# Plain weight pieces dealt in another order among the seven-product pairs of a one-core decoder block

## The chip, the core and the metric

The kernel runs on one core of a Trainium2 chip. The time is the device time of one execution in microseconds (us). Before the change it was 1505.64 us, the median of three runs (1503.54 to 1506.01).

The engines are named as in the profile: PE is TensorE (matmuls), DVE is VectorE, ACT is ScalarE, POOL is GpSimd, and SP is the engine whose queue issues the weight loads. Each engine works through its instructions in the order in which they were queued.

## The reference

A decoder block on 256 tokens of width 2048, in float32: one projection `w_in`, gated linear attention beside a short gated convolution, a merge by gates, an output projection, and a SwiGLU feed-forward part with 5632 hidden columns. What the change touches are the order of the gate projections and of the SwiGLU part.

```python
def hybrid_mixer(h, w_in, ...):
    proj = jnp.einsum('bsd,de->bse', h, w_in)
    (q, k, v, g_out, gk_low, gate_b, gate_c, xc, merge_a, merge_b) = jnp.split(proj, ...)
    ...
    y_a = o * jax.nn.silu(g_out)
    y_b = gate_b * causal_depthwise_conv(gate_c * xc, conv_w)
    merged = jax.nn.sigmoid(merge_a) * y_a + jax.nn.sigmoid(merge_b) * y_b
    return jnp.einsum('bse,ed->bsd', merged, w_out)

def swiglu(h, w_gate_up, w_down):
    gate, up = jnp.split(jnp.einsum('bsd,df->bsf', h, w_gate_up), [FFN_HIDDEN], axis=-1)
    return jnp.einsum('bsf,fd->bsd', jax.nn.silu(gate) * up, w_down)
```

## The kernel before

**Pieces.** All weights come as pieces of 128 x 1024 float32 (512 KB): two blocks of 128 rows by 512 columns. Each piece is split in two parts that TensorE takes at full speed: ScalarE rounds it (`hi`, line 238) and VectorE forms the remainder (`lo` = piece - `hi`, line 243). A product is then three matmuls (`mm3`, lines 347 to 349), with `lo` in the first. A *plain* piece is used for both halves of the 256 tokens: 2 blocks x 2 halves x 3 = 12 matmuls of 512 columns.

**Pairs.** Where two weight matrices meet the same input (`gc` and `xc` of the gates, `fg` and `fu` of SwiGLU), a pair of 512-column blocks is computed with seven products instead of eight. It has 28 pieces of 6 matmuls. `seven_list` gives their order: four quarters (q = 0 to 3) of five pieces `11`, `t1`, `t3`, `t2`, `t4`, and then eight last pieces `21` and `22`. The `t` pieces are sums of weight blocks: VectorE adds them (`sum_of`, lines 259 and 265), `t3`, `t2` and `t4` in place in the tile `x`; then the sum is rounded by ScalarE, and its `lo` formed by VectorE. The next sum in `x` needs the `lo` of the one before. `t2` is formed of what is there and needs no load. When a pair's products are complete, VectorE combines them with `v2`, `v3` and `u` (lines 424 to 437).

**Order.** `gates_list` and `hidden_list` write down the order of all pieces by hand. Among the 28 pieces of a pair stand plain pieces of other products. The gate pairs `gc0`, `gc1` and `gc2` have 24 plain pieces each (three products of eight), `gc3` has 32; the SwiGLU pairs of blocks 3, 5 and 7 have 16, those of blocks 4, 6, 9 and 10 have 15 (table `SEVENS`). The plain pieces there are, in order, those of `fg1`, `fu1`, `fg2`, `fu2`, of the down projection `dn0_0` to `dn1_3`, of `fg8`, `fu8`, and of `dn2_0` to `dn2_3`. The SwiGLU pair of block 0 has a table of its own.

`mixed` deals the plain pieces: one behind each `t` piece, then one behind each of the last eight, and round again while there are any. With 24 each quarter has four and each of the last eight one; with 16 or 15 the quarters take all, and the last eight stand in a row.

**Running ahead.** `take` emits the loading of five pieces ahead of their use (`LOOK`); there are five buffers for raw pieces, six for `hi`, five for `lo`. So VectorE can be some pieces ahead of TensorE. Steps that follow a product (evictions, transposes, the gates' elementwise work) are queued a given number of pieces later (`later`, `one_at_a_time`). Three PSUM banks serve the plain products (`lent`), two for one product, one for each half of the tokens; so a product that follows another takes over, for its second half, the bank of the other's first half, and it must have been drained by then: the gates `g` and `gb` by ScalarE (lines 929 and 935), `ma` and `mb` by ScalarE and VectorE (lines 919 and 920), the down projection by VectorE (`h`, line 1103). A scheduler may still move single instructions on their engines.

Of the kernel before, what the change touches and what calls it, by code (L numbers as in the profile page):

```python
# [19 lines left out]
KC = D // P  # L20
# [23 lines left out]
def plan():  # L44
# [28 lines left out]
GATES = (  # L73
    (None, ("g0",)),
    (("gc0", "xc0"), ("ma0", "gb0", "mb0")),
    (("gc1", "xc1"), ("g1", "ma1", "gb1")),
    (("gc2", "xc2"), ("mb1", "g2", "ma2")),
    (("gc3", "xc3"), ("gb2", "mb2", "g3", "ma3")),
    (None, ("gb3", "mb3")),
)  # L80
# [3 lines left out]
FIRST = {0: (6, 6, 8, 10, 12), 1: (14, 14, 16, 18, 20), 2: (22, 22, 23, 24, 26), 3: (28, 28, 29, 30, 31)}  # L84
FIRST_END = (31, 32)
SEVENS = ((3, 16), (4, 15), (5, 16), (6, 15), (7, 16), (9, 15), (10, 15))
PLAIN = (1, 2, (0, (0, 1, 2)), (1, (3, 4, 5)), 8, (2, (6, 7, 8)))


# [10 lines left out]
def seven_list(pair):  # L100

    out = [(what, q) for q in range(4) for what in ("11", "t1", "t3", "t2", "t4")]
    twos = (("21", 0), ("21", 1), ("22", 0), ("21", 2), ("22", 1), ("21", 3), ("22", 2), ("22", 3))
    return [(pair, e) for e in out + list(twos)]


def mixed(pair, eights, early=False):

    if pair is None:
        return eights  # L110
    sevens = seven_list(pair)
    sums = ("t1", "t3", "t2", "t4")
    gaps = [0] * len(sevens)
    rest = len(eights)
    while rest > 0:
        for some in (sums + ("11",) if early else sums, ("21", "22")):
            for n, (_, e) in enumerate(sevens):
                if e[0] in some and rest > 0:
                    gaps[n] += 1
                    rest -= 1  # L120
    out, put = [], 0
    for e, n in zip(sevens, gaps):
        out += [e] + eights[put:put + n]
        put += n
    return out


def gates_list():
    return [e for pair, keys in GATES
            for e in mixed(pair, [(key, k) for key in keys for k in range(0, KC, 2)], keys[0] == "gb2")]  # L130


def block_of(key):
# [3 lines left out]
def down_of(part, n, f):  # L137

    first = 4 * (f - PARTS[part][0])
    return [(f"dn{part}_{n}", k) for k in range(first, first + 4, PIECE // DOWN[part][n][1])]  # L140


def hidden_list():

    plain = []
    for what in PLAIN:
        if isinstance(what, tuple):
            part, fs = what
            plain += [e for n in range(len(DOWN[part])) for f in fs for e in down_of(part, n, f)]
        else:  # L150
            plain += [(f"{name}{what}", k) for name in ("fg", "fu") for k in range(0, KC, 2)]
    plain = [(f"wo{n}", k) for n in range(1, 4) for k in range(0, KC, 2)] + plain

    before = {(what, q): FIRST[q][n] for q in range(4) for n, what in enumerate(("11", "t1", "t3", "t2", "t4"))}
    pair = seven_list(("fg0", "fu0"))
    for n, (_, e) in enumerate(pair[20:]):
        before[e] = FIRST_END[0] + n * (FIRST_END[1] - FIRST_END[0]) // 7
    out, put = [], 0
    for key, e in pair:
        out += plain[put:before[e]] + [(key, e)]  # L160
        put = before[e]
    plain = plain[put:]
    for f, n in SEVENS:
        out += mixed((f"fg{f}", f"fu{f}"), plain[:n])
        plain = plain[n:]
    return out + plain

# [9 lines left out]
def stream_list():  # L177

    pieces = [(p[0], p[3]) for p in piece_list()]
    out = [e for e in pieces if e[0][0] in "kqv"] + gates_list() + [e for e in pieces if e[0] == "wo0"]  # L180
    return out + hidden_list() + down_list()
# [3 lines left out]
def block_kernel(ctx, tc, x, xt, cols_in, gkw_in, gku_in, gnw, conv_w, finw, w_in, w_out, w_gu, w_dn, out):  # L185
# [790 lines left out]

    xy = None
    steps = run(gates_list(), begin_gate)
    for n in steps:
        if n == 2:  # L980
# [82 lines left out]

    act = {}
    order = hidden_list()

    base = count["tick"]
# [178 lines left out]
```

## Time and profile before

| | |
|---|---|
| median of three runs | 1505.64 us |
| the profiled execution | 1504.77 us |
| its span, first to last instruction | 1503.1 us |
| granted TensorE clock, mean | 0.999 |
| ScalarE busy | 862.9 us (57%) |
| GpSimd busy | 37.9 us (3%) |
| HBM read | 351.03 MB |

A row of the profile names the line of the kernel, the engine, the operation, the tile that is written and those that are read, and where rows are grouped their count. In rows in order of time the first column is the start in us from the span's start and the second the duration in us. A matmul's row lasts longer than its share of the pace, since matmuls overlap: what counts is the distance from start to start. Behind an idle time stands, in square brackets, what ended it.

### The profile page before, as it was taken

How to read it: one execution, taken by the hardware profiler on the slowest of the kernel's cores; microseconds unless marked ns; L12 is line 12 of the kernel's file. 1: busy time of each engine (PE TensorE's matmuls, PEld its weight loads, DVE VectorE, ACT ScalarE, POOL GpSimd, SP SyncE). 2: the span in 40 equal slices, each digit the busy share in tenths (PEclk: the TensorE clock that was granted, in tenths of full speed). 3: DMA queues.
4: the chain of work that ended last, by engine and by line, in shares of the span. 5: the costliest groups of instructions: out<-in, count | busy, mean ns of one | idle time of the engine just before them, and what ended most of it. 6: DMA issues, size and time to landing. Idle time of an engine off the chain costs nothing.

```text
span 1503.1 us, 19369 instructions
## 1 busy us (share of the span) xinstructions
PE 1489.3 (99%) x7064; PEld 1243.9 (83%) x7064; DVE 1277.8 (85%) x1283; ACT 862.9 (57%) x977; POOL 37.9 (3%) x60
## 2 busy tenths in 40 slices
PE   9999999999999999999999999999999999999998
PEld 8989988888888888888888888888888788888887
DVE  6775869979979878966689999999999999999975
ACT  7773546655654654654556756655565556565553
POOL 0030000000000000000000000000000000000000
PEclk9999999999999999999999999999999999999999
DMA  9655557876886977786666777777877778777782
GB/s 354 200 170 179 171 170 265 273 230 232 281 259 235 304 227 252 258 264 209 217 220 214 238 246 251 255 261 220 272 238 239 253 263 269 246 263 231 235 287 94
DMA packets 100127, 358.57 MB, mean 239 GB/s; under 512 B 11492, under 2 KB 11620, under 8 KB 99904
## 3 DMA queue, kind: packets, MB, share of 16 engines
q1 hardware_dynamic: 96656, 346.73, 70.8%
q0 software_dynamic: 2800, 8.89, 2.2%
q10 hardware_dynamic: 576, 1.72, 0.3%
q8 instruction: 55, 0.90, 0.2%
q14 instruction: 40, 0.33, 0.1%
HBM read 351.03 MB, written 2.10 MB: 235 GB/s over the span
## 4 chain that ended last, share of the span: by engine, by line
PE 89%; DVE 5%; issue 3%; ACT 2%; DMA 1%; SPq 0%; DVEq 0%; ACTq 0%
PE fg L347 7%; PE fg L349 7%; PE fg L348 7%; PE dn L347 5%; PE dn L349 5%; PE dn L348 5%; PE gc L347 3%; PE gc L348 3%; PE gc L349 3%; DVE lo L243 3%; PE wo L347 2%; PE v L347 2%; PE v L348 2%; PE gb L347 2%; PE gb L349 2%
## 5 line engine op out<-in xcount | busy, mean ns | idle before, releaser
L243 DVE TENSOR_TENSOR lo<-raw,hi 128x1024 fp32r<-128x1024 f32 (+1 forms) x506 | 612.5, 1218 | 109.1 <-ACT hi L238 28.0
L238 ACT CAST hi<-raw 128x1024 fp32r<-128x1024 f32 (+1 forms) x506 | 523.8, 1047 | 270.8 <-PE gb L349 26.4
L238 ACT CAST hi<-x 128x1024 fp32r<-128x1024 f32 x144 | 151.6, 1053 | 276.2 <-DVE x L265 211.0
L243 DVE TENSOR_TENSOR lo<-x,hi 128x1024 fp32r<-128x1024 f32 x144 | 176.2, 1223 | 36.1 <-ACT hi L238 26.1
L347 PE MATMUL dn<-lo,acth 128*128 128x512 f32 (+1 forms) x368 | 140.8, 383 | 1.8 <-DVE h L1103 1.0
L349 PE MATMUL dn<-hi,acth 128*128 128x512 f32 (+1 forms) x368 | 139.9, 380 | 0.0
L348 PE MATMUL dn<-hi,actl 128*128 128x512 f32 (+1 forms) x368 | 139.8, 380 | 0.0
L265 DVE TENSOR_TENSOR x<-x,raw 128x1024 f32<-128x1024 f32 x96 | 117.1, 1220 | 14.7 <-DMA raw<-in_w_in_dram 9.3
L347 PE MATMUL fg<-lo,hh 128*128 128x512 f32 x288 | 112.4, 390 | 0.0
L348 PE MATMUL fg<-hi,hl 128*128 128x512 f32 x288 | 112.2, 389 | 0.0
L349 PE MATMUL fg<-hi,hh 128*128 128x512 f32 x288 | 112.2, 389 | 0.0
L347 PE MATMUL fg<-lo,sh 128*128 128x512 f32 x256 | 101.0, 395 | 0.0
L348 PE MATMUL fg<-hi,sl 128*128 128x512 f32 x256 | 99.9, 390 | 0.0
L349 PE MATMUL fg<-hi,sh 128*128 128x512 f32 x256 | 99.8, 390 | 0.0
L347 PEld LDWEIGHTS dn<-lo,acth 128*128 128x128 f32 x368 | 69.2, 188 | 16.2 <-DVE h L1103 2.3
L349 PEld LDWEIGHTS dn<-hi,acth 128*128 128x128 f32 x368 | 69.2, 188 | 13.3
L348 PEld LDWEIGHTS dn<-hi,actl 128*128 128x128 f32 x368 | 69.3, 188 | 12.9
L347 PEld LDWEIGHTS fg<-lo,hh 128*128 128x128 f32 x288 | 54.1, 188 | 11.8 <-DVE lo L243 0.5
L349 PEld LDWEIGHTS fg<-hi,hh 128*128 128x128 f32 x288 | 54.1, 188 | 11.2
L348 PEld LDWEIGHTS fg<-hi,hl 128*128 128x128 f32 x288 | 54.1, 188 | 11.1
L243 DVE TENSOR_TENSOR lo<-y,hi 128x1024 fp32r<-128x1024 f32 x48 | 58.5, 1219 | 5.4 <-ACT hi L238 2.4
L259 DVE TENSOR_TENSOR raw<-y,x 128x1024 f32<-128x1024 f32 x48 | 58.6, 1220 | 3.0 <-DMA y<-in_w_in_dram 1.5
(247 smaller groups left out, 3068.1 us busy)
## 6 DMA issues: line engine op xcount, KB each, us to landing
raw<-in_w_in_dram SPq DMA_DIRECT2D x254, 512.0 KB, 4.6
raw<-in_w_gu_dram SPq DMA_DIRECT2D x176, 512.0 KB, 4.4
raw<-in_w_dn_dram SPq DMA_DIRECT2D x88, 512.0 KB, 4.5
x<-in_w_gu_dram SPq DMA_DIRECT2D x32, 512.0 KB, 4.9
y<-in_w_gu_dram SPq DMA_DIRECT2D x32, 512.0 KB, 3.8
raw<-in_w_out_dram SPq DMA_DIRECT2D x32, 512.0 KB, 3.7
y<-in_w_in_dram SPq DMA_DIRECT2D x16, 512.0 KB, 4.2
x<-in_w_in_dram SPq DMA_DIRECT2D x16, 512.0 KB, 4.9
```

The costliest lines, as they stand in the source:

```text
L238: nc.scalar.copy(hi[:, ks, :], raw[:, ks, :])
L243: nc.vector.tensor_tensor(out=lo[:, ks, :], in0=raw[:, ks, :], in1=hi[:, ks, :].bitcast(F32), op=ALU.subtract)
L259: nc.vector.tensor_tensor(out=raw, in0=y, in1=held["x"], op=ALU.add)
L265: nc.vector.tensor_tensor(out=x, in0=x, in1=other, op=ALU.add)
L347: nc.tensor.matmul(ps, lhsT=sh, rhs=ml, start=first, stop=False, skip_group_check=onto)
L348: nc.tensor.matmul(ps, lhsT=sl, rhs=mh, start=False, stop=False, skip_group_check=onto)
L349: nc.tensor.matmul(ps, lhsT=sh, rhs=mh, start=False, stop=last, skip_group_check=onto)
```

## The change

The dealing is no longer done by one rule but by two tables of numbers, which say how many plain pieces each quarter gets; a quarter gives them out behind its pieces in the order `t1`, `t3`, `t2`, `t4`, `11`, `t3`, `t2`, and what is left is spread evenly over the last eight. In a gate pair with 24 the quarters get 5, 6, 6 and 5 instead of four each, and the last eight 2 instead of 8; with 32 the quarters get 7, 7, 7 and 6 and the last eight 5, where the quarters had 9, 5, 5 and 5 and the last eight 8. In a SwiGLU pair the quarters get 4, 4, 3 and 3 (16 plain pieces) or 4, 4, 3 and 2 (15), and the last eight 2, where they had none. The two stand in the middle of the last eight and at the end. The pair of block 0 and all that is outside the pairs stay.

```diff
+GATES_QUADS = {24: (5, 6, 6, 5), 32: (7, 7, 7, 6)}
+SEVENS_QUADS = {15: (4, 4, 3, 2), 16: (4, 4, 3, 3)}
...
+def dealt(pieces, quads):
+
+    out = []
+    for n in quads:
+        places = [0] * 5
+        for i in (1, 2, 3, 4, 0, 2, 3)[:n]:
+            places[i] += 1
+        out += places
+    rest = pieces - sum(quads)
+    return out + [(i + 1) * rest // 8 - i * rest // 8 for i in range(8)]
+
+
-def mixed(pair, eights, early=False):
+def mixed(pair, eights, gaps):
 
     if pair is None:
         return eights
-    sevens = seven_list(pair)
-    sums = ("t1", "t3", "t2", "t4")
-    gaps = [0] * len(sevens)
-    rest = len(eights)
-    while rest > 0:
-        for some in (sums + ("11",) if early else sums, ("21", "22")):
-            for n, (_, e) in enumerate(sevens):
-                if e[0] in some and rest > 0:
-                    gaps[n] += 1
-                    rest -= 1
+    assert sum(gaps) == len(eights)
     out, put = [], 0
-    for e, n in zip(sevens, gaps):
+    for e, n in zip(seven_list(pair), gaps):
         out += [e] + eights[put:put + n]
         put += n
     return out
...
-        out += mixed((f"fg{f}", f"fu{f}"), plain[:n])
+        out += mixed((f"fg{f}", f"fu{f}"), plain[:n], dealt(n, SEVENS_QUADS[n]))
```

Two places show what becomes of this on the engines. The first is VectorE's queue in the fourth quarter of the SwiGLU pair of block 6, from the addition of `t3` on: the tile `x` holds the sums `t3`, `t2` and `t4` one after the other, `lo` from `raw` is that of a plain piece, and `h` is the draining of `dn1_1`. Before:

```order
L265 TENSOR_TENSOR x_9835<-x_9835,raw_9867 128x1024
L243 TENSOR_TENSOR lo_9872<-raw_9849,hi_9850 128x1024
L243 TENSOR_TENSOR lo_9884<-x_9835,hi_9870 128x1024
L243 TENSOR_TENSOR lo_9901<-raw_9880,hi_9881 128x1024
L265 TENSOR_TENSOR x_9835<-x_9835,y_9817 128x1024
L243 TENSOR_TENSOR lo_9914<-x_9835,hi_9899 128x1024
L243 TENSOR_TENSOR lo_9927<-raw_9910,hi_9911 128x1024
L265 TENSOR_TENSOR x_9835<-x_9835,raw_9922 128x1024
L1103 TENSOR_TENSOR h_6297<-dn1_1_0_9743,h_6297 128x512
L1103 TENSOR_TENSOR h_6297<-dn1_1_1_9744,h_6297 128x512
L243 TENSOR_TENSOR lo_9947<-x_9835,hi_9925 128x1024
```

With the change (the lines of the file are nine higher):

```order
L274 TENSOR_TENSOR x_9817<-x_9817,raw_9849 128x1024
L252 TENSOR_TENSOR lo_9872<-x_9817,hi_9852 128x1024
L252 TENSOR_TENSOR lo_9883<-raw_9868,hi_9869 128x1024
L274 TENSOR_TENSOR x_9817<-x_9817,y_9805 128x1024
L252 TENSOR_TENSOR lo_9892<-x_9817,hi_9881 128x1024
L274 TENSOR_TENSOR x_9817<-x_9817,raw_9894 128x1024
L1112 TENSOR_TENSOR h_6297<-dn1_1_0_9743,h_6297 128x512
L1112 TENSOR_TENSOR h_6297<-dn1_1_1_9744,h_6297 128x512
L252 TENSOR_TENSOR lo_9909<-x_9817,hi_9897 128x1024
```

The `lo` of `t3` now stands directly behind the addition that makes `t3`, where a plain piece's `lo` stood between them; the plain piece between `t2` and `t4` is gone, so that the addition of `t4` follows the `lo` of `t2` at once.

The second place is TensorE's queue in the gate pair `gc0`, where the plain product `ma0` ends (`ma0_1` is its second half of the tokens). Before:

```order
L347 MATMUL ma0_1_2352<-lo_2523,xh_108 128x512
L348 MATMUL ma0_1_2352<-hi_2508,xl_109 128x512
L349 MATMUL ma0_1_2352<-hi_2508,xh_108 128x512
L347 MATMUL gc0_0_2321<-lo_2543,xh_108 128x512
L348 MATMUL gc0_0_2321<-hi_2521,xl_109 128x512
L349 MATMUL gc0_0_2321<-hi_2521,xh_108 128x512
```

With the change:

```order
L356 MATMUL ma0_1_2341<-lo_2499,xh_108 128x512
L357 MATMUL ma0_1_2341<-hi_2484,xl_109 128x512
L358 MATMUL ma0_1_2341<-hi_2484,xh_108 128x512
L356 MATMUL gb0_0_2577<-lo_2516,xh_108 128x512
L357 MATMUL gb0_0_2577<-hi_2496,xl_109 128x512
L358 MATMUL gb0_0_2577<-hi_2496,xh_108 128x512
```

Before, two pieces of the pair (`11` and `t1` of its third quarter) stood between `ma0` and the next plain product `gb0`; now `gb0` begins directly behind it. The same holds for `g1` and `ma1` in `gc1`, `mb1` and `g2` in `gc2`, and `g3` and `ma3` in `gc3`.

More of the change, by code (lines that the diff above doesn't have):

```diff
@@ L128, in gates_list @@
 def gates_list():
-    return [e for pair, keys in GATES
-            for e in mixed(pair, [(key, k) for key in keys for k in range(0, KC, 2)], keys[0] == "gb2")]
+    out = []
+    for pair, keys in GATES:
+        eights = [(key, k) for key in keys for k in range(0, KC, 2)]
+        out += mixed(pair, eights, dealt(len(eights), GATES_QUADS[len(eights)] if pair else ()))
+    return out
 def block_of(key):
```

## The prediction

> **What bounds the kernel now.** I read the busy times first, then the chain that ended last, then one row per pair, and then single instructions.
>
> ```profile
> span 1503.1 us, 19369 instructions
> ...
> PE 1489.3 (99%) x7064; PEld 1243.9 (83%) x7064; DVE 1277.8 (85%) x1283; ACT 862.9 (57%) x977; POOL 37.9 (3%) x60
> ...
> PE 89%; DVE 5%; issue 3%; ACT 2%; DMA 1%; SPq 0%; DVEq 0%; ACTq 0%
> ```
>
> TensorE (PE) holds 89% of the chain, and VectorE (DVE) 5%: there are places where PE waits for it. The change leaves every matmul as it is, so only PE's stalls can move. To size them I take the pace from PE's rows in order of time: the starts of two pieces of the pair `gc1` with a plain piece of `g1` behind the first.
>
> ```profile
> 349.38 0.39 PE L347 MATMUL gc<-lo,sh 128*128 128x512 f32 x1
> ...
> 353.46 0.39 PE L347 MATMUL gc<-lo,sh 128*128 128x512 f32 x1
> ```
>
> These 18 matmuls take 4.08 us: 2.72 for the 12 of a plain piece, 1.36 for the 6 of a pair piece. Below is the table of stretches, each from the start of one pair to that of the next: four gate pairs, then the SwiGLU pairs of blocks 3, 4, 5, 6, 7, 9 and 10.
>
> ```profile
> core 0: us, PE busy (x) PEld busy (x) DVE busy (x) ACT busy (x) POOL busy (x), PEclk, DMA share, GB/s
> 227.01:330.57 103.56, 103.56 (x457) 85.51 (x456) 89.90 (x81) 62.54 (x65) 0.00 (x0) 1.00 0.78 255
> 330.57:435.81 105.24, 104.89 (x465) 86.35 (x464) 95.91 (x90) 60.81 (x64) 5.01 (x9) 1.00 0.78 257
> 435.81:542.03 106.22, 105.15 (x465) 86.07 (x464) 93.92 (x87) 60.02 (x63) 4.95 (x9) 1.00 0.78 255
> 542.03:668.20 126.17, 126.17 (x561) 104.25 (x560) 105.47 (x97) 70.58 (x74) 5.07 (x10) 1.00 0.81 256
> 865.02:948.55 83.53, 83.53 (x377) 69.14 (x376) 77.98 (x74) 50.73 (x54) 0.00 (x0) 1.00 0.77 250
> 948.55:1028.89 80.34, 80.34 (x361) 66.50 (x360) 75.80 (x72) 45.53 (x48) 0.00 (x0) 1.00 0.76 251
> 1028.89:1112.03 83.14, 83.14 (x373) 68.68 (x372) 77.56 (x75) 46.84 (x50) 0.00 (x0) 1.00 0.76 252
> 1112.03:1193.34 81.31, 80.74 (x357) 65.80 (x356) 76.65 (x74) 45.34 (x48) 0.00 (x0) 1.00 0.77 252
> 1193.34:1277.32 83.98, 83.10 (x370) 68.29 (x368) 78.89 (x76) 46.72 (x50) 0.00 (x0) 1.00 0.77 251
> 1277.32:1358.53 81.21, 81.21 (x365) 66.73 (x364) 76.28 (x72) 48.39 (x52) 0.00 (x0) 1.00 0.79 254
> 1358.53:1440.32 81.79, 80.42 (x358) 65.92 (x356) 76.69 (x75) 46.29 (x49) 0.00 (x0) 1.00 0.74 241
> ```
>
> The pieces alone need 28 x 1.36 plus 2.72 for each plain piece: 103.36 us with 24, 125.12 with 32, 81.60 with 16, 78.88 with 15. Records beyond the pieces' own matmuls are transposes; block 4's row (361 - 348 = 13 of them, 80.34 - 78.88 = 1.46 us) prices them at 0.11 us, if it has no stall. The rest of each stretch is stall: 0.1, 0.9, 1.9 and 0.1 in the gates (2.9 together), and 0.1, 0, 0.1, 1.4, 1.3, 0.5 and 1.8 in SwiGLU (5.2, of which 5.1 from block 5 on). So **8 us is all that a better order could win here**. The clock is 1.00 in all rows. PE's waits name the releasers:
>
> ```profile
> PE dn L347 <- DVE h L1103: 1.0, 2, 0.5
> PE trb L597 <- DVE sg L1062: 0.9, 1, 0.9
> PE dn L347 <- DVE lo L243: 0.8, 1, 0.8
> PE ma L347 <- ACT ya L929: 0.6, 1, 0.6
> ```
>
> They are VectorE's results three times. In SwiGLU it is busy 76 to 79 us of 80 to 84, and it also waits:
>
> ```profile
> DVE lo L243 <- ACT hi L238: 22.3, 33, 1.2
> ```
>
> That is the view of VectorE's waits from 865 to 1440 us. One such wait, in block 10, in order of time:
>
> ```profile
> 1414.10 1.22 DVE L265 TENSOR_TENSOR x<-x,y 128x1024 f32<-128x1024 f32 x1
> 1416.49 1.23 DVE L243 TENSOR_TENSOR lo<-x,hi 128x1024 fp32r<-128x1024 f32 x1 [1.17 <-ACT hi L238]
> 1417.63 1.22 DVE L243 TENSOR_TENSOR lo<-raw,hi 128x1024 fp32r<-128x1024 f32 x1
> ```
>
> Wide operations start 1.14 us apart (1416.49 to 1417.63). Where the low part of a sum is queued directly behind the addition that makes it, ScalarE's rounding stands between, and they start 2.39 apart: **1.25 us of VectorE is lost at each such place**. The chain that ended last runs through this very place, up to PE's stall at `dn2_3`:
>
> ```profile
> 1414.10 1.23 DVE x L265
> 1415.41 1.06 ACT hi L238
> ...
> 1420.65 0.50 PE dn L347
> ```
>
> How far VectorE is ahead of PE shows where a low part ends and PE first reads it, here at block 5's start and in block 10's first quarter:
>
> ```profile
> 1025.13 1.22 DVE L243 TENSOR_TENSOR lo<-y,hi 128x1024 fp32r<-128x1024 f32 x1
> ...
> 1370.97 1.23 DVE L243 TENSOR_TENSOR lo<-x,hi 128x1024 fp32r<-128x1024 f32 x1
> ```
>
> ```profile
> 1028.66 0.39 PE L347 MATMUL fg<-lo,hh 128*128 128x512 f32 x1
> ...
> 1372.41 0.40 PE L347 MATMUL fg<-lo,hh 128*128 128x512 f32 x1
> ```
>
> It is 1028.66 - 1026.35 = 2.3 us ahead, then 1372.41 - 1372.20 = 0.2: nothing is left over. From block 5 on both engines are at their limit.
>
> **The change, part by part.** Nothing is added or removed; the same 28 pair pieces and 15, 16, 24 or 32 plain ones stand in another order, with their transfers on SP's queue and their roundings on ScalarE's. No transfer should come to bind: a plain piece brings one load to 2.72 us of PE, and putting two among the last eight pieces of a SwiGLU pair, one load to 1.36 us each, thins out the densest place. The rows' DMA share stays near 0.77.
>
> *Gates.* Six of the eight plain pieces among a pair's last eight go into its quarters (two of the eight in `gc3`, beside a new deal between its quarters). A plain piece gives PE 2.72 us for 1.14 of VectorE, so VectorE gains 1.6 us of lead with each, in the quarters where the 2.9 us arose. I leave 0.4 of it. In return four pairs now end one plain product and begin the next without a pair piece between them (`ma0` to `gb0` is shown with the change), so the bank that the second needs must be drained in 2.72 us of PE (half of the last piece and half of the next first one) instead of at least 4.08. From below that costs nothing: the last row quoted in this part has two such neighbours, 214 matmuls in 48.00 us. From above it is the 0.6 us of `ma` waiting for `ya`, four times. Nearer is the free one, but with VectorE less busy there; I take 0.5 in all. **Sum for the gates -2.9 + 0.4 + 0.5 = -2.0 us** (-2.9 to -0.1).
>
> ```profile
> 664.00:712.00 48.00, 48.00 (x214) 39.67 (x213) 30.93 (x29) 23.64 (x25) 3.11 (x6) 1.00 0.76 224
> ```
>
> *SwiGLU.* Two plain pieces per pair go from the third and fourth quarter to the last eight. Products end elsewhere: between `dn1_1` and `dn1_2`, and `dn2_2` and `dn2_3`, there are six pair pieces instead of one, so the waits for `h` go. What is late next is the low parts. In VectorE's order I counted the low parts queued directly behind their own addition, for blocks 3, 4, 5, 6, 7, 9, 10: now 0, 0, 3, 3, 3, 1, 3, with the change 0, 2, 5, 5, 4, 5, 5, that is 13 and 26. The rows shown with the change are of block 6: a plain piece's low part that stood between the addition and its low part now stands ahead of both, and nothing fills the wait.
>
> For the five pairs from block 5 on: PE needs 411.4 us less the 5.1 of stall, 406.3. VectorE is busy 386.1 and idle 25.3, of which 13 x 1.25 = 16.3 at those places and 9.1 for other causes. How much of these 9.1 stays nothing shows: none, or all; I take 6.0, 1.2 a pair, since VectorE was ahead in block 9 alone. With the change it needs 386.1 + 24 x 1.25 + 6.0 = 422.1, 15.8 more than PE. Against this stands its lead. Two plain pieces before block 5's start give 3.2 us more, the two new waits in block 4 take some; with 2.5 more it starts 4.8 ahead, and 0.2 of that is no use. Stalls: 15.8 - 4.6 = 11.2, where 5.1 are now. **SwiGLU +6.1 us** (+0.1 with none of the other idle time, +9.2 with all).
>
> At this point a rule can be weighed: PE at 99% of the page against PEld at 83% and VectorE at 85%. By the Trainium skill ("Perfetto Trace Analysis", section "Identifying the Most-Contended Engine"), matmul busy time is a poor measure and TensorE is to be judged by its weight loads; VectorE would then be the most contended engine throughout, and the sum would be that of the last rival, not +4.1. The trace does not agree for the whole kernel: 214 matmuls ran unbroken in 48.00 us with VectorE busy 30.93. From block 5 on it nearly does.
>
> **Sum:** -2.0 + 6.1 = +4.1 us. The profiled execution took 1504.77 us (span 1503.1), 0.87 below the median 1505.64 and within the three runs. 1508.9 for it, **1509.7 in terms of the median**; by the bounds -2.8 to +9.1, 1502.8 to 1514.7.
>
> **Rivals.**
> - *The spread wins, faster.* The order now starves VectorE among the last eight pieces and the next first quarter; two plain pieces there raise its lowest lead (0.2 us) by up to 3.2, and the added waits fall where it would have waited for a free buffer anyway. Gates -2.5, SwiGLU stalls down to 1: -6.6, 1499. It decides if an added wait costs under 0.88 us instead of 1.25: 11 x 0.37 = 4.1, the whole sum. For it: blocks 3 and 4 do not stall. Against: from block 5 on VectorE has nothing spare. The Trainium skill ("Perfetto Trace Analysis", section "Optimization Strategy" under "Identifying Performance Opportunities") says that interleaving stretches with different limiting engines may help, which is what is done here; the trace neither confirms nor refutes it. 0.16.
> - *It evens out.* If other idle time is 0.3 us a pair: 386.1 + 30 + 1.5 - 406.3 - 4.6 = 6.7, so +1.6 and -2.0: 1505.2. 0.24.
> - *The gates lose too.* All four neighbours cost 0.6: 1511.6. 0.05.
> - *VectorE binds throughout.* No lead hides anything, and all 13 added waits are paid in full: 13 x 1.25 = 16.3, less 2.0: 1519.9. The busy times of blocks 5 to 10 speak for it, the unstalled blocks 3 and 4 against it. 0.03.
>
> **How the numbers follow.** My case gets 0.52. About 0.2% (3 us) is what a measurement of this kernel can tell from no change. Slower by more: 0.52 + 0.05 + 0.03 = 0.60; within: 0.24; faster: 0.16. The range 1502.0 to 1515.0 takes in the bounds and the case that evens out; it leaves out most of the faster case and the last one.
>
> **What would show it.** Right: 1.2 us waits of `lo` for `hi` about twice as many from 865 to 1440 us; stalls gone from the second and third gate stretch; the stretches of blocks 6, 9 and 10 longer by 1 to 3 us each, with PE waiting for `lo`; no wait of `dn` for `h` at `dn1_2` and `dn2_3`. Wrong: SwiGLU stretches that shrink although the waits double (the lead covers them), or a stall at `gb0`, `ma1`, `g2` or `ma3`.

## The result, and the profile after

The changed kernel took 1513.92 us (median of six runs, 1510.61 to 1516.48), the kernel before 1505.62 (six runs beside it, 1502.53 to 1506.50): a ratio of 1.0058, 95% interval 1.0042 to 1.0074. It is 8.3 us slower, twice the +4.1 of the forecast. The profiled execution took 1513.34 us, 8.57 more than that of before; its span is 1511.6. The head of its page, busy time by engine:

```profile
span 1511.6 us, 19346 instructions
...
PE 1491.7 (99%) x7064; PEld 1243.4 (82%) x7064; DVE 1278.4 (85%) x1283; ACT 864.2 (57%) x977; POOL 38.0 (3%) x60
```

No engine has more work: VectorE is busy 1278.4 us where it was 1277.8. Below is the table of stretches for the changed kernel, in the same order as that of before: the four gate pairs, then the SwiGLU pairs of blocks 3, 4, 5, 6, 7, 9 and 10.

```profile
core 0: us, PE busy (x) PEld busy (x) DVE busy (x) ACT busy (x) POOL busy (x), PEclk, DMA share, GB/s
226.74:330.51 103.77, 103.65 (x457) 85.51 (x456) 88.99 (x80) 62.44 (x64) 0.00 (x0) 1.00 0.77 248
330.51:434.84 104.33, 104.33 (x466) 86.38 (x464) 96.41 (x90) 61.19 (x64) 5.02 (x9) 1.00 0.82 260
434.84:540.43 105.59, 104.66 (x465) 86.30 (x464) 95.20 (x88) 60.48 (x63) 4.97 (x9) 1.00 0.82 256
540.43:666.52 126.09, 126.09 (x562) 104.40 (x560) 105.35 (x97) 71.78 (x74) 5.09 (x10) 1.00 0.81 257
863.40:947.02 83.62, 83.62 (x378) 69.07 (x376) 77.77 (x74) 48.39 (x51) 0.00 (x0) 1.00 0.75 249
947.02:1029.13 82.11, 80.65 (x361) 66.42 (x360) 76.46 (x73) 47.16 (x51) 0.00 (x0) 1.00 0.76 247
1029.13:1112.70 83.57, 83.44 (x374) 68.60 (x372) 76.47 (x73) 46.91 (x50) 0.00 (x0) 1.00 0.78 249
1112.70:1197.85 85.15, 81.43 (x357) 65.62 (x356) 78.16 (x77) 45.34 (x48) 0.00 (x0) 1.00 0.74 241
1197.85:1281.03 83.18, 83.18 (x369) 68.12 (x368) 77.49 (x74) 46.34 (x49) 0.00 (x0) 1.00 0.77 255
1281.03:1364.96 83.93, 82.04 (x365) 66.49 (x364) 75.98 (x73) 47.62 (x52) 0.00 (x0) 1.00 0.74 243
1364.96:1448.04 83.08, 80.70 (x354) 65.31 (x352) 75.99 (x73) 45.08 (x48) 0.00 (x0) 1.00 0.72 234
```

The four gate stretches together take 439.78 us, where they took 441.19: 1.4 us won. Taking off the pieces and 0.11 us for each transpose, as for the kernel before, the SwiGLU rows leave 0, 1.8, 0.4, 5.3, 0.6, 3.2 and 3.5 us of stall, together 14.8 where there were 5.2. The loss is in the pairs with 15 plain pieces (blocks 4, 6, 9, 10). From the start of pair `fg3` to the first piece of the last down projection the kernel before took 586.67 us and this one 596.48; this **SwiGLU stretch** (+9.8) is the yardstick for the experiments.

The same views of waits as before, PE's and then the first line of VectorE's, over that part of the changed kernel:

```profile
PE fg L356 <- DVE lo L252: 4.8, 5, 1.3
PE fg L356 <- DVE u L435: 1.5, 1, 1.5
PE dn L356 <- DVE actl L609: 1.4, 2, 1.2
PE trb L606 <- DVE sg L1071: 1.1, 2, 0.6
```

```profile
DVE lo L252 <- ACT hi L247: 36.1, 36, 1.3
```

PE's waits for `h` are gone; it waits for VectorE everywhere. VectorE's waits of `lo` for `hi` rose from 22.3 to 36.1 us. The instructions in order of time show how: VectorE, and then PE, at the end of the fourth quarter of block 6, the place whose queue is printed with the change.

```profile
1165.19 1.22 DVE L274 TENSOR_TENSOR x<-x,raw 128x1024 f32<-128x1024 f32 x1
1167.61 1.22 DVE L252 TENSOR_TENSOR lo<-x,hi 128x1024 fp32r<-128x1024 f32 x1 [1.20 <-ACT hi L247]
...
1169.89 1.22 DVE L274 TENSOR_TENSOR x<-x,y 128x1024 f32<-128x1024 f32 x1
1172.28 1.23 DVE L252 TENSOR_TENSOR lo<-x,hi 128x1024 fp32r<-128x1024 f32 x1 [1.17 <-ACT hi L247]
...
1175.94 1.23 DVE L252 TENSOR_TENSOR lo<-x,hi 128x1024 fp32r<-128x1024 f32 x1
```

```profile
1177.22 0.50 PE L356 MATMUL fg<-lo,hh 128*128 128x512 f32 x1 [1.28 <-DVE lo L252]
```

Two additions are each followed by their own `lo`, 2.4 us from start to start; the third `lo` ends at 1177.17 and PE, which has been idle for 1.28 us, goes on at once.

### The profile page after: what moved, and what is told of

It reads as the page before. It is cut to its first block, busy times and chain, and to the rows that moved or that the text cites. A ratio compares the mean times of both kernels' runs of the same rounds, so it can differ in the third digit from the quotient of the medians.

```text
span 1511.6 us, 19346 instructions
## 1 busy us (share of the span) xinstructions
PE 1491.7 (99%) x7064; PEld 1243.4 (82%) x7064; DVE 1278.4 (85%) x1283; ACT 864.2 (57%) x977; POOL 38.0 (3%) x60
## 4 chain that ended last, share of the span: by engine, by line
PE 72%; DVE 5%; issue 2%; ACT 1%; DMA 1%; DVEq 0%; ACTq 0%
PE fg L356 7%; PE fg L358 7%; PE fg L357 7%; PE dn L356 4%; PE dn L358 4%; PE dn L357 4%; PE gc L358 3%; PE gc L357 3%; PE gc L356 3%; DVE lo L252 3%; PE wo L356 2%; PE wo L357 2%; PE wo L358 2%; PE gb L356 2%; PE gb L357 2%
## 5 line engine op out<-in xcount | busy, mean ns | idle before, releaser
L358 PEld LDWEIGHTS dn<-hi,acth 128*128 128x128 f32 x368 | 69.2, 188 | 13.3
```

The lines of the kernel that those rows point to most:

```text
L358: nc.tensor.matmul(ps, lhsT=sh, rhs=mh, start=False, stop=last, skip_group_check=onto)
```

## The experiments

My theory: each *place* (a low part queued directly behind its own addition) takes 1.25 us from VectorE, and the deal is slower because it makes 26 places out of 13. The main rival: the dealing itself costs the time, since in a last quarter with two or three plain pieces PE eats pair pieces faster than VectorE can form them, waits or not. Places are counted in VectorE's queue for blocks 4 to 10 throughout.

**The halves apart.** `e1_gates` keeps the old deal in SwiGLU, `e2_swiglu` keeps it in the gates (the lists written out are the old gaps).

```diff
-SEVENS_QUADS = {15: (4, 4, 3, 2), 16: (4, 4, 3, 3)}
+SEVENS_QUADS = {15: (4, 4, 4, 3), 16: (4, 4, 4, 4)}
```

```diff
-dealt(len(eights), GATES_QUADS[len(eights)] if pair else ())
+[0, 1, 1, 1, 1] * 4 + [1] * 8 if len(eights) == 24 else [2, 2, 2, 2, 1] + [1] * 23
```

> Only the gate pairs get the new deal; the SwiGLU pairs keep the old one. Theory (an added place where a low part waits for the rounding of its own sum costs VectorE 1.25 us, and the gates win by more lead): about 1.5 us faster than before, gate stretches together 1.4 us shorter, a stall of 0.9 us where g2 follows mb1. Rival (the gates' neighbours cost more than the traces of one run show): no gain or a loss of up to 1 us.

> Only the SwiGLU pairs get the new deal; the gates keep the old one. Theory: 9 to 10 us slower than before, all of it from block 4 on, with PE waiting for lo. If the two halves add up, this and the gates alone give the whole change (+8.3 us). Rival (the change's time comes from the gates, or from code after them): less than 7 us slower.

The gates alone: 1503.38 us against 1504.20, ratio 0.9993 (0.9984 to 1.0002). The whole interval is within 2.4 us of gain and 0.3 us of loss; the time alone does not show the gain, the stretches do (439.2 us together, 2.0 less than before). The stall at `g2` did not come in the profiled execution; a wait of 0.5 us at `gb0`, another of the four neighbours, did. SwiGLU alone: 1514.30 us, ratio 1.0071 (1.0058 to 1.0084), 10.1 us slower. The two add up to 9.3 against 8.3 measured for the whole, within their intervals. The loss is all SwiGLU's.

**Without places.** `e3_apart` is the changed kernel, `e4_before_apart` the kernel before, both with the sums written so that none needs the `lo` of the last one to be finished:

```diff
-        if halfway and halfway[-1][0] is x:
-            finish_low()
-        other = y if what == "t2" else fetch(two if what == "t3" else one, 4 * q + 2)
-        nc.vector.tensor_tensor(out=x, in0=x, in1=other, op=ALU.add)
-        return x
+        if what == "t2":
+            nc.vector.tensor_tensor(out=x, in0=held["t3"], in1=y, op=ALU.add)
+            return x
+        raw = fetch(two if what == "t3" else one, 4 * q + 2)
+        nc.vector.tensor_tensor(out=raw, in0=x, in1=raw, op=ALU.add)
+        held[what] = raw
+        return raw
```

> The changed kernel, but the sums t3 and t4 are written over the loaded piece and t2 alone into x, so that no sum waits for the low part of the one before; in VectorE's queue no low part stands directly behind its own addition any more (26 places before block 11 in SwiGLU become 0). PE's order of pieces stays. Theory (the places cost the time): VectorE needs 386 + 6 = 392 us of 406 from block 5 on, so the 14.8 us of SwiGLU stalls fall below 3; about 12 us faster than the changed kernel, 3 to 6 us faster than before. Rival (thin quarters: with two or three plain pieces in the last quarters PE eats pair pieces faster than VectorE forms them, waits or not): the stalls of the 15-piece pairs stay, at most 4 us faster than the changed kernel. Second rival (a loaded piece stays longer in its buffer, so the next load comes late): slower, with DMA as releaser of VectorE's waits.

> The kernel before with the same edit of the sums (13 places become 0). Theory: the 5.1 us of SwiGLU stalls from block 5 on mostly go, 3 to 5 us faster than before. Rival thin quarters: the same as before within 1 us. Rival late loads: slower.

Both were slower in all: 1516.44 us, ratio 1.0087 (1.0073 to 1.0101), and 1513.26, ratio 1.0055 (1.0041 to 1.0069). As totals these expectations failed. By stretches two things happened at once. In SwiGLU the theory held: PE has not one wait in `e3_apart`, and its SwiGLU stretch is 581.75 us, 14.7 less than that of the changed kernel and 4.9 less than before; that of `e4_before_apart` is 584.06, 2.6 less than before. In the gates the second rival held: their four stretches took 459.2 us instead of 439.8. VectorE's waits there, in `e3_apart` and in the changed kernel:

```profile
DVE raw L275 <- DMA raw<-in_w_in_dram: 34.9, 15, 4.5
```

```profile
DVE x L274 <- DMA raw<-in_w_in_dram: 7.1, 5, 3.9
```

By the edit, a loaded piece that also holds its sum keeps one of the five raw buffers until the `lo` is formed, and the additions wait 34.9 us for late loads where they waited 7.1; that the one brings the other fits, but no run tested it by itself (with more buffers, say). Why SwiGLU, with fewer plain pieces per pair, bears it (3.5 us of such waits) wasn't tried.

**Places without the deal.** `e8_before_places` is the kernel before; at 13 sums the pending `lo` is put ahead of the addition, so that nothing is left to stand behind it; the order of the low parts after them shifts too, and 30 places are counted where 13 were. PE's pieces stay in their order, but for a few transposes and pair pieces that the scheduler moved.

```diff
+PLACES = [(f, (what, q)) for f in (4, 5, 6, 7, 9, 10) for q in (1, 2) for what in ("t3",)] + [(9, ("t4", 1))]
...
+                if (key, k0) in AT_ONCE and halfway:
+                    finish_low()
                 raw = sum_of(key, *k0)
...
+        if halfway and halfway[-1][2:] in AT_ONCE:
+            finish_low()
```

> The kernel before, in which at the sums t3 of the second and third quarter of blocks 4 to 10 (and t4 of block 9's second) the low part that waits to be formed is queued ahead of the addition instead of behind it; by VectorE's queue 30 places instead of 13, no piece dealt otherwise. Theory (a place costs 1.25 us of VectorE): 386.1 + 28 x 1.25 + 6.0 = 427.1 us for blocks 5 to 10, 20.8 more than PE, with 0 to 2 us of lead: 19 to 21 us of stall where 5 were, so 14 to 16 us slower than before. Rival (the dealing itself costs the time, by thin quarters or by products that end elsewhere): within 2 us of before.

1524.07 us, ratio 1.0123 (1.0105 to 1.0140): 18.5 us slower, more than the 14 to 16 expected; its profiled execution, with 1520.6, is 15.8 above that of before. VectorE's waits of `lo` for `hi` over its SwiGLU stretch:

```profile
DVE lo L245 <- ACT hi L240: 45.4, 48, 1.8
```

Over the same stretch of the kernel before they are 24.2 us: 21.2 more for 17 places, 1.25 us each. With the plain pieces where they always were, these places alone cost more than the change with its 13 more. The rival (within 2 us) falls.

**The deal without places.** `b1_apart_new_deal` is the changed kernel, and `b2_apart_old_deal` the same with the old deal in SwiGLU; the sums are written apart, as above, only in blocks 3 to 10:

```diff
+        if one[:2] == "fg" and one != "fg0":
+            if what == "t2":
...
         if halfway and halfway[-1][0] is x:
```

> The changed kernel, with the sums written apart (t3 and t4 over the loaded piece) in the SwiGLU pairs of blocks 3 to 10 alone; 0 places there, the gates and block 0 as in the changed kernel. Theory: no stall in SwiGLU (the trace of the changed kernel with all sums apart had none there), so the 14.8 us go: 1499 (1497.5 to 1501). Rival (the late loads that cost that kernel its gates come here too, once the gates no longer fall behind): over 1503.

> As the last, with the old deal in SwiGLU. Theory: with no places, the plain pieces among the last eight are a gain of 2 us (the SwiGLU of the two kernels with all sums apart took 581.8 and 584.1 us): 1501 (1499.5 to 1503). Rival (the deal does not matter without places): the same as the last within 0.5 us.

1498.36 us, ratio 0.9956 (0.9944 to 0.9969), and 1500.04, ratio 0.9969 (0.9957 to 0.9981). Both as the theory said, and both faster than the two kernels of the study. In `b1_apart_new_deal` the pair of block 6 runs without a stall:

```profile
1111.25:1191.13 79.88, 79.88 (x358) 66.01 (x356) 75.92 (x73) 45.37 (x46) 0.00 (x0) 1.00 0.74 255
```

79.88 us where the changed kernel took 85.15, with the pieces in the same order but for a few matmuls that the scheduler moved. VectorE's waits over its SwiGLU stretch have another head:

```profile
DVE lo L252 <- PE dn L364: 9.5, 12, 1.6
DVE lo L252 <- ACT hi L247: 6.7, 21, 0.6
DVE lo L252 <- PE fg L364: 5.0, 6, 1.3
DVE lo L252 <- PE fu L364: 4.6, 5, 1.1
```

VectorE now waits for PE to free a buffer, 19.1 us in three of these lines: it is ahead. And the new deal is then no loss but the better one, by 1.0 us in the SwiGLU stretches (582.33 and 583.29 us), where PE's wait for `h` (1.2 us) is left in the old deal; the medians differ by 1.7 us. All runs of the one lie below all runs of the other, though the intervals of the ratios overlap.

**Between.** `e5_fifteens_old` gives the old deal back to the pairs of 15; `e6_one_back` puts one of the two plain pieces back into the quarters of every pair.

```diff
-SEVENS_QUADS = {15: (4, 4, 3, 2), 16: (4, 4, 3, 3)}
+SEVENS_QUADS = {15: (4, 4, 4, 3), 16: (4, 4, 3, 3)}
```

```diff
-SEVENS_QUADS = {15: (4, 4, 3, 2), 16: (4, 4, 3, 3)}
+SEVENS_QUADS = {15: (4, 4, 3, 3), 16: (4, 4, 4, 3)}
```

> The changed kernel with the old deal for the pairs of 15 plain pieces (blocks 4, 6, 9, 10); those of 16 (blocks 3, 5, 7) keep the new one. 18 places instead of 26. Theory: 386.1 + 17 x 1.25 + 6.0 = 413.4 for blocks 5 to 10, 7.1 more than PE, less 3 to 5 us of lead: 2 to 4 us of stall; 9 to 12 us faster than the changed kernel, 0 to 2 us faster than the gates alone. Rival (each pair dealt anew costs the same, about 1.4 us): 5 to 6 us faster than the changed kernel, some 4 us slower than the gates alone.

> The changed kernel with one of the two plain pieces among the last eight put back into the last quarters in every SwiGLU pair (4, 4, 3, 3 of 15 and 4, 4, 4, 3 of 16): 23 places instead of 26, and in the pairs of 15 a plain piece behind the last t2 again. Theory (places): 3 x 1.1 to 1.25, 3 to 4 us faster than the changed kernel, and the 1.5 us for which PE waits for u in block 4 go: 4 to 6 us in all, 1508 to 1510. Rival (both pieces of a pair cost alike, each about 0.7 us for 14 of them): 7 x 0.7, also 5 us faster, but with the wait for u still there. So the trace decides here, not the time.

`e5_fifteens_old`: 1506.37 us, ratio 1.0007 (0.9998 to 1.0016); between the theory's number and the rival's, a miss of both. `e6_one_back`: 1511.94 us, ratio 1.0053 (1.0038 to 1.0067), hardly faster than the change (1.0058), where 4 to 6 us were expected: a miss. PE's wait for `u` in block 4 went as expected (that stretch fell from 82.11 to 80.34), and blocks 6 and 9 fell by 2.6 and 1.2 us, but block 7 grew by 2.1, and block 10 with what follows it in the SwiGLU stretch by 1.5. So a single place doesn't have a fixed price; only over a run of pairs is there an average. The kernels so far, side by side:

| kernel | deal in SwiGLU | places | SwiGLU stretch, us |
|---|---|---|---|
| e3_apart, b1_apart_new_deal | new | 0 | 581.75, 582.33 |
| e4_before_apart, b2_apart_old_deal | old | 0 | 584.06, 583.29 |
| before, e1_gates | old | 13 | 586.67, 586.38 |
| e5_fifteens_old | new in the 16s | 18 | 587.81 |
| e6_one_back | one piece back | 23 | 594.84 |
| after, e2_swiglu | new | 26 | 596.48, 598.02 |
| e8_before_places | old | 30 | 602.30 |

From 0 to 18 places the stretch grows by some 5 us; from 18 to 30 by 14.5, on average 1.21 us a place, though unevenly: two kernels with 26 places differ by 1.5 us. What absorbs the first shows in VectorE's waits for PE to free a buffer: 19.1 us in `b1_apart_new_deal`, 5.3 in the kernel before, 3.4 in the changed one. The first places fall into time in which VectorE would have waited for PE; for the others hardly any of it is left.

**Two more tries on the best kernel.** `b3_gates_free` deals the gates so that no plain product follows another directly, `b4_one_back` puts one plain piece back in SwiGLU, both on top of `b1_apart_new_deal`.

```diff
-GATES_QUADS = {24: (5, 6, 6, 5), 32: (7, 7, 7, 6)}
+GATES_QUADS = {24: (6, 5, 6, 5), 32: (7, 7, 6, 7)}
```

```diff
-SEVENS_QUADS = {15: (4, 4, 3, 2), 16: (4, 4, 3, 3)}
+SEVENS_QUADS = {15: (4, 4, 3, 3), 16: (4, 4, 4, 3)}
```

> The kernel with the sums apart in SwiGLU and the new deal there (1498.4 us), with gate quarters of 6, 5, 6, 5 (24 plain pieces) and 7, 7, 6, 7 (32): no plain product of the gates follows another without a pair piece between them. Theory (each such neighbour can stall at the drained bank): the waits of g and gb for sb and ya (0.7 and 0.6 us in that kernel's trace) vanish, 0.5 to 1.5 us faster. Rival (the other order of the quarters costs VectorE as much): the same within 0.5 us.

> The same kernel (sums apart, new deal, 1498.4 us) with SwiGLU quarters of 4, 4, 3, 3 and 4, 4, 4, 3, so one plain piece among the last eight. Theory: without places nothing but the wait for u in block 4 (0.4 us) and that for h (1.2 us in the old deal's trace) is left, and one piece behind the last t2 removes the first without bringing back the second: the same or up to 0.7 us faster. Rival (VectorE needs both pieces there): 0.5 to 1.5 us slower, half of the way to the old deal.

`b4_one_back`: 1498.85 us, ratio 0.9965 (0.9952 to 0.9978), the same as `b1_apart_new_deal`, with neither wait left. `b3_gates_free`: 1504.69 us, ratio 1.0000 (0.9991 to 1.0010), 6 us slower than its parent, a clear miss. The wait of `gb` for `ya` (0.6 us in the parent) is gone, as expected. The loss is one place, PE's first matmul of `g2`'s second half, and VectorE's queue ahead of it:

```profile
472.73 0.79 PE L364 MATMUL g<-lo,xh 128*128 128x512 f32 x1 [4.06 <-DVE sb L937]
```

```profile
466.32 1.22 DVE L921 TENSOR_TENSOR u<-u,taps 128x1024 f32<-128x1024 f32 x1
467.46 1.22 DVE L252 TENSOR_TENSOR lo<-x,hi 128x1024 fp32r<-128x1024 f32 x1
468.59 1.22 DVE L921 TENSOR_TENSOR u<-u,u 128x1024 f32<-128x1024 f32 x1
469.73 1.22 DVE L282 TENSOR_TENSOR x<-x,raw 128x1024 f32<-128x1024 f32 x1
470.86 1.22 DVE L252 TENSOR_TENSOR lo<-raw,hi 128x1024 fp32r<-128x1024 f32 x1
472.00 1.28 DVE L937 TENSOR_TENSOR sb<-sb,mb 128x512 f32<-128x512 f32 x2
```

PE is free at 468.5 and waits for the draining of `mb1` (`sb`), which stands behind the convolution's operations on `u` in VectorE's queue and starts at 472.00. A pair piece does stand between `mb1` and `g2` here. The wait comes here from where the draining stands in VectorE's queue, behind the convolution, and not from two plain products side by side. Nor is a pair piece between them any safeguard at `gb0`: in `e4_before_apart` two of them stand between `ma0` and `gb0`, and PE waits 3.2 us for `ya` there.

## Why the prediction was right, and where its size was off

*The gates.* Right in direction, -1.4 us in the profiled execution against -2.0. Over the seven traces with this deal and the sums of the gates in place the four stretches take 439.70 us on average, over the three with the old deal 441.22: 1.5 us won. The stall of the second stretch went; the third kept 0.9 us, PE waiting for `sb` at `g2`, one of the four neighbours priced at 0.5 us in all. In the same seven traces PE waits 0 to 1.9 us at `gb0` and `g2` together, 0.9 on average, and not once at `ma1` and `ma3`: the price was too low by half. Its reason was not right either, as `b3_gates_free` shows: at `g2` VectorE's queue decides, not the neighbour.

*The places.* Right: 13 and 26, at 1.25 us each. `e8_before_places` slows the kernel by them alone, `b1_apart_new_deal` keeps the deal, takes them away, and the stalls are gone. The rival that the spread wins named the condition under which it would (a place under 0.88 us), and with no places it does win.

*The other idle time of VectorE.* Held. To form the low parts of all pieces from the first of block 5 to the last of block 10, VectorE took 419.2 us in the changed kernel: 384.4 busy, 28.5 idle at the 24 places (1.19 each, the part of the 1.25 that shows as idle), and 6.3 idle otherwise (10.3 in the kernel before), where 6.0 were taken. PE without its stalls took 405.9. So VectorE needed 13.3 us more than PE, where 15.8 were forecast, and PE stalled for 13.0.

*The lead: the step that failed.* "Two plain pieces before block 5's start give 3.2 us more, the two new waits in block 4 take some; with 2.5 more it starts 4.8 ahead." Of that, 4.6 was to come off the stalls. It started 1028.90 - 1025.73 = 3.2 ahead, 0.9 more than before. The rows, VectorE's and PE's, at the starts of blocks 5 and 10 in the changed kernel:

```profile
1024.51 1.22 DVE L252 TENSOR_TENSOR lo<-y,hi 128x1024 fp32r<-128x1024 f32 x1
...
1361.20 1.23 DVE L252 TENSOR_TENSOR lo<-y,hi 128x1024 fp32r<-128x1024 f32 x1
```

```profile
1028.90 0.39 PE L356 MATMUL fg<-lo,hh 128*128 128x512 f32 x1
...
1364.74 0.39 PE L356 MATMUL fg<-lo,hh 128*128 128x512 f32 x1
```

The two new waits in block 4 are not what took the rest: `b1_apart_new_deal`, without a single place, is 3.2 ahead at block 5's start too. Nor is the lead spent once and for all. At the starts of blocks 6, 7, 9 and 10 VectorE is 1.4, 2.2, 2.9 and 2.3 ahead again, and 2.8 at block 10's end; within each of these pairs, and within block 5's, the lead falls to 0.1 and PE stalls. So from block 5's start to block 10's end it hid 3.2 - 2.8 = 0.4 us, not 4.6.

And block 4, which I had at no stall, lost 1.8 us, 1.5 of it here, on VectorE and then on PE:

```profile
1012.30 0.68 DVE L434 TENSOR_TENSOR v<-fg,v 128x512 f32<-128x512 f32 x1
1014.64 1.23 DVE L252 TENSOR_TENSOR lo<-raw,hi 128x1024 fp32r<-128x1024 f32 x1 [1.65 <-PE fg L356]
1015.78 0.68 DVE L435 TENSOR_TENSOR u<-fg,v 128x512 f32<-128x512 f32 x1
```

```profile
1016.52 0.50 PE L356 MATMUL fg<-lo,sh 128*128 128x512 f32 x1 [1.46 <-DVE u L435]
```

VectorE was too far ahead here: the next low part waits 1.65 us for PE to free its buffer, and `u`, which PE needs for its next `22`, stands behind it. Before, a plain piece behind the last `t2` gave 2.72 us for this; with one piece put back (`e6_one_back`) the wait is gone. So lead can't be stored at will: with five buffers of low parts, what a plain piece gave beyond them was spent waiting here. (More buffers were not tried.) Of the 3.7 us by which SwiGLU came out above +6.1, block 4's stall makes 1.8, and the stalls from block 5 on, 13.0 where 11.2 were forecast, make 1.8: about 4.2 us of lead that hid nothing, less the 2.5 us by which VectorE's need was put too high.

*The sum.* -2.0 + 6.1 was forecast; -1.4 + 9.8 came: 8.57 us in the profiled executions with what lies outside, 8.3 in the medians. 1513.92 lies within the range, near its upper end, where all the other idle time was to be paid; it was the lead instead. That the two errors from block 5 on partly cancel is luck. What should have shown it came: no wait for `h`, the waits for `hi` up by 13.8 us (those above 1 us from 13 to 27), blocks 6, 9 and 10 longer by 3.8, 2.7 and 1.3 us, the first by more than the 1 to 3 forecast. The stall at `g2`, named as a sign against, came too, at 0.9 us.

## What to carry to other kernels

Before moving work between stretches, read what it separates on the engines that feed the bottleneck: a piece that looks like ballast for TensorE may be what fills a wait between two other engines on VectorE's queue. If an in-place chain makes that wait, break the chain first (here by writing two of three sums elsewhere); the deal that lost 8 us then became the better one. But a buffer held longer has its price where loads are dense, so break it only there where the profile shows loads to spare.

## What the runs showed of the hardware

A stall of PE may cost more than its length. After the 4.06 us at `g2` in `b3_gates_free` the granted clock in the rows of three windows is 0.50, 0.67 and 1.00:

```profile
472.70:476.00 3.30, 3.27 (x8) 2.59 (x9) 3.30 (x4) 1.53 (x3) 0.52 (x1) 0.50 0.24 57
476.00:480.00 4.00, 4.00 (x14) 3.16 (x13) 4.00 (x4) 0.79 (x1) 0.00 (x0) 0.67 0.88 270
480.00:484.00 4.00, 4.00 (x19) 3.32 (x18) 3.94 (x5) 2.00 (x2) 0.00 (x0) 1.00 0.82 293
```

From 473.33 to 478.45 there are twelve steps of 0.43 us from matmul to matmul instead of 0.23, and one of 0.60 and 0.33 at the ends: 2.9 us more. The stretch took 111.45 us against 104.59 in `e1_gates`; these 6.9 us are the stall and the slow matmuls behind it. In `e3_apart` and `e4_before_apart` it followed stalls of 2.44, 3.10, 3.22 and 4.63 us, for 7 to 12 steps; after stalls of 2.27 us and less the pace was 0.23 at once (the two longest of these, 2.04 and 2.27, are in the same two kernels, behind the gates). The Trainium skill ("TensorE: Matmul & The Clock Gate", section "HAM oscillation — how this bites in real kernels") gives as rule no idle gaps of TensorE above about 3.4 us; the loss of pace agrees, but here gaps of 2.44 to 3.22 us already brought it. Part of the gates' loss in `e3_apart` is this; the short waits of SwiGLU do not pay it.
